# Moving the first norm's scale ahead of the last row blocks of the queries' projection, and ScalarE's first table load ahead of the first tile

## The chip, the core and the metric

The kernel runs on one core of a Trainium2 chip. The metric is the device time of one execution in microseconds (us). The engines are TensorE (PE, matrix multiply; PEld is its weight load), VectorE (DVE), ScalarE (ACT), GpSimd (POOL) and SyncE (SP, which here only issues DMAs). Each engine works through its own instructions in order and waits on semaphores for the others.

## The reference

Two layers of a decoder trunk on a 512 x 2048 input. Only the opening of the first layer matters here: a root-mean-square norm, one wide projection whose columns are split into parts, and a rotary embedding of the queries `b_q` and the keys `b_k`.

```python
def rms_norm(x, w, eps=NORM_EPS):
    xf = x.astype(jnp.float32)
    xf = xf * lax.rsqrt(jnp.mean(xf * xf, axis=-1, keepdims=True) + eps)
    return xf.astype(x.dtype) * w

h = rms_norm(x, pre_w)
proj = h @ w_in
...
qb = apply_rope(b_q.reshape(B, S, SW_HEADS, SW_HEAD_DIM), cos4, sin4)
kb = apply_rope(b_k.reshape(B, S, SW_KV_HEADS, SW_HEAD_DIM), cos4, sin4)
lam = (jnp.exp(jnp.sum(lq1 * lk1)) - jnp.exp(jnp.sum(lq2 * lk2)) + lam_init)
```

## The kernel before

Every product is made of three matmuls, since both factors are held as a high and a low part (`three`, L309): high x high, high x low, low x high. The high part of a weight tile, `whi`, is a cast on ScalarE (L151); the low part, `wlo`, is a subtraction (L152), on VectorE for even row blocks and on POOL for odd ones. The input is treated alike: `act_hi` on ScalarE (L154), `act_lo` on VectorE (L155). Rings limit how far this runs ahead: three raw weight tiles of two row blocks each, and four `whi` and `wlo`, so the cast of a row block needs the matmuls of the fourth block before it to be done.

The first layer opens with the queries' projection (L617). `gemm_tok` runs over 16 row blocks k of 128 rows of `w_in`; for each it adds to four PSUM banks `g` of 128 tokens x 512 columns, 12 matmuls to a block, so 192 in all. `sweep` (L316) orders them: `tail=2` holds the last two blocks back and runs them as one group, bank by bank, so that bank 0 is complete before the others. `before=start` calls `start(k)` (L1062) ahead of each block. It loads the input tiles `xt` by DMA on SP's queue (limited by N_LOAD), splits them (`take`, limited by N_TAKE), squares them on ScalarE and adds the squares up in `ssum` on VectorE (`square`, L1044), and moves the rotary tables forward by a step of VectorE work (`angles`, L206 to L238).

The norm's scale is not applied to the input but to what comes out. When the 16th square is added, `first_scale` (L1055) is queued on the lanes, a small planner that `sweep` calls after each group; it yields L_FIRST first, which puts it behind the last group. It sums `ssum` over partitions by four small products on TensorE (`css`, `col_sums` L454), and VectorE makes `r_in` by a Newton iteration (`rsqrt`, L157). Then VectorE scales the rotary tables (L281) and rotates the queries bank by bank (`rotate_q`, L249 to L259); L253 is the last reader of a bank. The next product (L624: the rotary key, keys and values, 16 blocks of 320 columns, here called kv0 to kv15) needs the same four banks: its first group takes kv0 and kv1 bank by bank, six matmuls to a bank, and so follows the rotations. Between the rotations and the rest of that product stands `layer_constants` (L484): four small DMAs of `lam_in` on SP's queue, products and sums on VectorE (L498, L499) and an exponential on ScalarE (L500), behind which later casts of `kv` tiles are queued.

ScalarE's first instruction that needs a function table is the split of the first input tile (L154).

Of the kernel before, what the change touches and what calls it, by code (L numbers as in the profile page):

```python
# [12 lines left out]
F32 = mybir.dt.float32  # L13
F32R = mybir.dt.float32r
I32 = mybir.dt.int32
AF = mybir.ActivationFunctionType
# [3 lines left out]
P = 128  # L20
# [12 lines left out]
B_Q, B_K, B_G = 2048, 3072, 3328  # L33
# [75 lines left out]
def trunk(ctx: ExitStack, tc: tile.TileContext, ins, inv_freq, out):  # L109
    nc = tc.nc  # L110
    PS = bass.MemoryType.PSUM
    const = ctx.enter_context(tc.tile_pool(name="const", bufs=1))
# [20 lines left out]
    A = nc.scalar  # L133
# [32 lines left out]
        return y  # L166


    ident = const.tile([P, P], F32, name="ident")
    make_identity(nc, ident)  # L170
    act_hi = const.tile([P, 2, KT, 256], F32R, name="act_hi")
    act_lo = const.tile([P, 2, KT, 256], F32R, name="act_lo")
    ones_r = const.tile([P, P], F32R, name="ones_r")
    ones_f = const.tile([P, 2], F32, name="ones_f")
    nc.gpsimd.memset(ones_f, 1.0)
    A.activation(ones_r, ident, AF.Copy, scale=0.0, bias=1.0)
    causal = const.tile([P, S], F32, name="causal")
    nc.gpsimd.memset(causal, 0.0)
    nc.gpsimd.affine_select(out=causal[:, 384:512], in_=causal[:, 384:512], pattern=[[-1, P]],
# [96 lines left out]
    def scaled_tables(r, half, to):  # L276

        mm_ = slice(2 * half, 2 * half + 2)
        rb = r[:, mm_].rearrange("p (m o) -> p m o", o=1).broadcast_to([P, 2, 64])
        for src, dst in zip(tabs, to):  # L280
            V.tensor_tensor(dst[:, mm_, :], src[:, mm_, :], rb, op=ALU.mult)  # L281
# [4 lines left out]
    def stream(w, segs, nk, C, rows=0, before=None):  # L286

        for k0 in range(0, nk, 2):
            raw = wraw.tile([P, 2, S], F32, name="raw", tag="raw")
            c = 0  # L290
            for off, width in segs:
                for j, n in ((0, 1), (1, 1)) if opening[0] else ((0, 2),):
                    nc.sync.dma_start(
                        out=raw[:, j:j + n, c:c + width],
                        in_=w[rows + (k0 + j) * P:rows + (k0 + j + n) * P, off:off + width].rearrange(
                            "(k p) c -> p k c", p=P))
                opening[0] = False
                c += width
            for i in range(2):
                if before:  # L300
                    before(rows // P + k0 + i)
                hi = wsp.tile([P, S], F32R, name="whi", tag="whi")[:, 0:C]
                lo = wsp.tile([P, S], F32R, name="wlo", tag="wlo")[:, 0:C]
                with (tc.high_priority() if ahead[0] or last_rows[0] else nullcontext()):
                    split(hi, lo, raw[:, i, 0:C], behind=behind[0], E=nc.gpsimd if ahead[0] or (i and not last_rows[0]) else V)
                behind[0] = False
                yield k0 + i, hi, lo

    def three(out_ap, a, b, first, last):  # L309

        (ah, al), (bh, bl) = a, b
        mm(out_ap, ah, bh, start=first, stop=False)
        mm(out_ap, ah, bl, start=False, stop=False)
        mm(out_ap, al, bh, start=False, stop=last)

    def sweep(tiles, nk, jobs, after=None, tail=2, head=True):  # L316

        def run(group):  # L320
            for job in jobs:
                for n, t in group:
                    job(t, n == 0, n == nk - 1)
                if fine[0] and job is not jobs[-1]:
                    lanes.tick()
            for n, t in group:
                if after:
                    after(n)
            lanes.tick()

        held = []
        for n, t in enumerate(tiles):
            held.append((n, t))
            if (n == 0 and head) or nk - tail <= n < nk - 1:
                continue
            run(held)
            held = []
# [12 lines left out]
    def gbanks(n):  # L350
        return [psg.tile([P, S], F32, name="g", tag="g") for _ in range(n)]

    def gemm_tok(block, w, segs, C, nk=KT, ms=range(NB), kruns=None, before=None, tail=2, head=True):

        ps = gbanks(len(ms))

        def tiles():
            for k0, cnt in kruns or ((0, nk),):
                for k, hi, lo in stream(w, segs, cnt, C, k0 * P, before):
                    yield k0 + k, hi, lo  # L360

        sweep(tiles(), nk, [lambda t, a, z, p=p, m=m: three(p[:, 0:C], block(t[0], m), t[1:], a, z)
                            for p, m in zip(ps, ms)], tail=tail, head=head)
        return ps
# [119 lines left out]
    def layer_constants(l, cols):  # L484
        c = dict(qnw=cols[:, KT:KT + 4], kvnw=cols[:, KT + 4:KT + 8])
        lam_init = 0.8 - 0.6 * math.exp(-0.3 * l)
        sub = layer_c.tile([P, 1], F32, name=f"sub{l}")
        V.tensor_scalar(sub, cols[:, KT + 8:KT + 9], 0.5 * (1.0 - lam_init), None, op0=ALU.mult)
        sink = layer_c.tile([P, 16], F32, name=f"sink{l}")
        nsink = layer_c.tile([P, 16], F32, name=f"nsink{l}")  # L490
        late(nc.sync.dma_start(out=sink, in_=ins["sink_logits"][l].partition_broadcast(P)))
        V.tensor_scalar(nsink, sink, -1.0, None, op0=ALU.mult)
        lt = slot("lam_in", "et", shape=(P, 4, 64))
        for i, n in enumerate(("q1", "k1", "q2", "k2")):
            late(nc.sync.dma_start(out=lt[:, i, :], in_=ins["diff_lambda_" + n][l].partition_broadcast(P)))
        d, junk = sm("lam_d", 2), slot("lam_j", "et", shape=(P, 64))
        for i in range(2):
            V.tensor_tensor(junk, lt[:, 2 * i, :], lt[:, 2 * i + 1, :], op=ALU.mult)  # L498
            V.tensor_reduce(d[:, i:i + 1], junk, axis=AX.X, op=ALU.add)  # L499
        A.activation(d, d, AF.Exp)  # L500
        nlam = layer_c.tile([P, 1], F32, name=f"nlam{l}")
        V.tensor_tensor(nlam, d[:, 1:2], d[:, 0:1], op=ALU.subtract)
        V.tensor_scalar(nlam, nlam, -lam_init, None, op0=ALU.add)
        c.update(sub=sub, sink=sink, nsink=nsink, nlam=nlam)
        return c
# [54 lines left out]
    def layer(l, pre, norms, r_in, start=None):  # L560
# [3 lines left out]
        w_in, w_out, w_uq, w_ukv = (ins[n][l] for n in ("w_in", "w_out", "w_uq", "w_ukv"))  # L564
# [12 lines left out]
        def fed(half, k):  # L577
            tasks, done, _ = norms[half]
            lanes.finish_until(lambda: min(done) > k // 4,
                               lambda: any(t is q for t in tasks for q in lanes.queue))  # L580
# [14 lines left out]
        def rotate_q(ps, m):  # L595
            d = slot("q_rot", "rot")
            rope(d, ps, m, 8, rtabs)
            return d
# [15 lines left out]

        kv_segs = [(C_KR, 64), (B_K, 256)]
        if start:
            ps = gemm_tok(act_block, w_in, [(B_Q, 512)], 512, before=start, head=False)  # L617
            lanes.finish(*norms)
            for half in range(2):
                scaled_tables(r_in, half, rtabs)  # L620
            for m in range(NB):
                qt[0][m] = rotate_q(ps[m], m)
            c = layer_constants(l, pre)
            kd = key_tiles(gemm_tok(act_block, w_in, kv_segs, 320, tail=3), range(NB), None)  # L624
            keys += [lanes.add(key_half, half, kd[2 * half:2 * half + 2]) for half in range(2)]
        for half in range(0 if start else 2):
            ms = (2 * half, 2 * half + 1)
            ps = gemm_tok(act_block, w_in, kv_segs, 320, ms=ms, before=lambda k: fed(half, k))
# [6 lines left out]
            ps = gemm_tok(act_block, w_in, [(B_Q, 512)], 512, ms=ms)  # L635
# [100 lines left out]
        ps = gemm_tok(act_block, w_in, [(B_Q + 512, 512)], 512)  # L736
# [43 lines left out]
        ps = gemm_T(act, w_in, [(C_Q, S)])  # L780
        qh, ql, ssum = latent(ps, c["qnw"])
        scales = [lanes.add(q_scale, ssum)]
        ps = gemm_T(act, w_in, [(C_KV, S)])
# [4 lines left out]
        ps = gemm_tok(lambda k, m: cut((qh[k], ql[k]), m), w_uq, [(192 * h + 128, 64) for h in range(4)], 256, nk=4)  # L788
# [154 lines left out]
        for h in range(4):  # L943
            ps = gemm_tok(
                act_block, w_in, [(A_K + 128 * h, 128), (A_Q + 128 * h, 128), (A_V + 128 * h, 128)], 384)
# [8 lines left out]
            for m in range(NB):  # L954
                A.activation(raw[:, :, m, :], ps[m][:, 0:384].rearrange("p (k c) -> p k c", k=3), AF.Copy,
                             scale=r_in[:, m:m + 1])
# [96 lines left out]
            norms.append(lanes.add(first_scale))  # L1053

    def first_scale(lane):  # L1055
        yield L_FIRST
        ms = sm("ms")
        V.tensor_scalar(ms, col_sums(bank("css", lane), ssum), 1.0 / DM, EPS, op0=ALU.mult, op1=ALU.add)
        V.tensor_copy(r_in, rsqrt(ms, "rin"))
        yield 0.0  # L1060

    def start(k):  # L1062
        while loaded[0] < min(2 * k + 3, k + N_LOAD, KT):
            load(loaded[0])
            loaded[0] += 1
        while taken[0] < min(k + 1 if k < 2 else 2 * k, k + N_TAKE, KT):
            take(taken[0])
# [22 lines left out]
L_SW = 5.0  # L1090
L_MLA = 7.0
L_DA = 4.5
N_LOAD = 6
N_TAKE = 3
L_FIRST = 2.0
L_KEYS = 5.0
L_SCALE = 1.0
L_FEED = 4.0
# [32 lines left out]
```

## Time and profile before

| | |
|---|---|
| median of 3 runs | 1769.45 us (1768.54 to 1769.94) |
| profiled execution, time | 1767.51 us |
| its span, first to last instruction | 1765.7 us |
| mean granted TensorE clock | 0.993 |
| TensorE busy with matmuls | 1719.0 us, 97% |
| VectorE, ScalarE, POOL busy | 51%, 46%, 42% |

The engine with the most work is TensorE; what is left to gain is in the stretches where it stands still or runs at a lower clock. A timeline row gives start and duration in us, engine, line, operation, result and operands; a bracket at its end tells how long the engine had been idle and what ended the wait. Durations of neighbouring instructions overlap a little, so the distance between two starts is what an instruction costs its engine.

### The profile page before, as it was taken

How to read it: one execution, taken by the hardware profiler on the slowest of the kernel's cores; microseconds unless marked ns; L12 is line 12 of the kernel's file. 1: busy time of each engine (PE TensorE's matmuls, PEld its weight loads, DVE VectorE, ACT ScalarE, POOL GpSimd, SP SyncE). 2: the span in 40 equal slices, each digit the busy share in tenths (PEclk: the TensorE clock that was granted, in tenths of full speed). 3: DMA queues.
4: the chain of work that ended last, by engine and by line, in shares of the span. 5: the costliest groups of instructions: out<-in, count | busy, mean ns of one | idle time of the engine just before them, and what ended most of it. 6: DMA issues, size and time to landing. Idle time of an engine off the chain costs nothing. (4 is left out here: it accounts for less than half of the span.)

```text
span 1765.7 us, 24988 instructions
## 1 busy us (share of the span) xinstructions
PE 1719.0 (97%) x8776; PEld 1478.0 (84%) x8776; DVE 899.5 (51%) x2216; ACT 803.5 (46%) x1744; POOL 746.6 (42%) x630
## 2 busy tenths in 40 slices
PE   8899999999999999999989999999999999999997
PEld 6888888888999988887777888888889999888885
DVE  8445625653435767202785563365625367671035
ACT  6244525544334445235554453355434344552353
POOL 3243443443444444457434434433434434444550
PEclk9999999999999999999999999999999999999998
DMA  6332232232323233336765323222323322332366
GB/s 199 81 95 78 84 101 84 64 104 72 107 78 80 72 111 115 110 107 193 230 188 168 96 84 96 84 84 75 98 68 111 83 71 74 118 131 87 117 207 222
DMA packets 155918, 195.42 MB, mean 111 GB/s; under 512 B 22144, under 2 KB 81552, under 8 KB 155792
## 3 DMA queue, kind: packets, MB, share of 16 engines
q1 hardware_dynamic: 152384, 183.31, 34.8%
q0 software_dynamic: 3264, 10.51, 1.7%
q8 instruction: 69, 1.13, 0.3%
q14 instruction: 57, 0.47, 0.1%
q10 hardware_dynamic: 144, 0.01, 0.0%
HBM read 181.20 MB, written 12.58 MB: 110 GB/s over the span
## 5 line engine op out<-in xcount | busy, mean ns | idle before, releaser
L152 POOL TENSOR_TENSOR wlo<-raw,whi 128x512 fp32r<-128x512 f32 (+3 forms) x576 | 721.9, 1261 | 932.3 <-ACT whi L151 905.0
L151 ACT CAST whi<-raw 128x512 fp32r<-128x512 f32 (+2 forms) x672 | 388.9, 583 | 626.5 <-PE g L142 481.4
L142 PE MATMUL g<-whi,act_hi 128*128 128x512 f32 (+2 forms) x1408 | 525.1, 373 | 12.5 <-ACT whi L151 6.9
L142 PE MATMUL g<-wlo,act_hi 128*128 128x512 f32 (+2 forms) x1408 | 520.2, 369 | 13.3 <-DVE wlo L152 11.8
L142 PE MATMUL g<-whi,act_lo 128*128 128x512 f32 (+2 forms) x1408 | 517.7, 368 | 0.0
L142 PE MATMUL g<-act_hi,whi 128*128 128x512 f32 x768 | 310.9, 405 | 1.7 <-DVE vl L155 0.6
L142 PEld LDWEIGHTS g<-wlo,act_hi 128*128 128x128 f32 x1408 | 266.4, 189 | 54.2 <-DVE wlo L152 16.9
L142 PEld LDWEIGHTS g<-whi,act_hi 128*128 128x128 f32 x1408 | 266.4, 189 | 48.8 <-ACT whi L151 7.4
L142 PE MATMUL g<-act_hi,wlo 128*128 128x512 f32 x768 | 303.7, 395 | 0.1
L142 PE MATMUL g<-act_lo,whi 128*128 128x512 f32 x768 | 303.4, 395 | 0.0
L142 PEld LDWEIGHTS g<-whi,act_lo 128*128 128x128 f32 x1408 | 266.1, 189 | 34.6
L142 PEld LDWEIGHTS g<-act_hi,wlo 128*128 128x128 f32 x768 | 144.3, 188 | 35.1 <-POOL wlo L152 0.5
L142 PEld LDWEIGHTS g<-act_hi,whi 128*128 128x128 f32 x768 | 144.6, 188 | 32.5 <-DVE vl L155 1.5
L142 PEld LDWEIGHTS g<-act_lo,whi 128*128 128x128 f32 x768 | 144.7, 188 | 29.1
L152 DVE TENSOR_TENSOR pTl<-pT,pTh 128x512 fp32r<-128x512 f32 (+2 forms) x112 | 68.2, 611 | 96.4 <-ACT pTh L151 96.2
L987 DVE TENSOR_TENSOR ob<-g,post_norm_w 128x512 f32<-128x512 f32 x32 | 22.1, 690 | 177.4 <-ACT sq L985 177.4
L152 DVE TENSOR_TENSOR wlo<-raw,whi 128x512 fp32r<-128x512 f32 (+1 forms) x96 | 66.2, 695 | 90.1 <-ACT whi L151 90.0
L151 ACT CAST pTh<-pT 128x512 fp32r<-128x512 f32 (+2 forms) x112 | 58.6, 525 | 46.0 <-PE pT L146 45.1
L446 DVE CUSTOM_DVE_ANT_0 p<-sc,causal 128x128 f32<-128x128 f32 (+3 forms) x96 | 46.0, 479 | 33.9 <-PE sc L142 33.9
L146 PE MATMUL pT<-ident,p 128*128 128x128 f32 x384 | 61.0, 274 | 1.4 <-DVE p L852 1.4
L661 ACT ACTIVATE p<-p,nm 128x256 f32<-128x256 f32 (+1 forms) x128 | 59.9, 469 | 0.0
L448 ACT ACTIVATE p<-p,nm 128x128 f32<-128x128 f32 (+3 forms) x64 | 36.0, 562 | 49.7 <-DVE nm L447 49.7
(236 smaller groups left out, 2009.7 us busy)
## 6 DMA issues: line engine op xcount, KB each, us to landing
raw<-w_in SPq DMA_DIRECT2D x135, 512.0 KB, 3.7
raw<-w_out SPq DMA_DIRECT2D x96, 512.0 KB, 3.8
raw<-w_in SPq DMA_DIRECT2D x192, 128.0 KB, 2.4
raw<-w_in SPq DMA_DIRECT2D x26, 256.0 KB, 3.0
xt<-x_t SPq DMA_DIRECT2D x16, 256.0 KB, 6.8
y_spill<-gate POOLq DMA_DIRECT2D x16, 256.0 KB, 2.9
raw<-w_ukv SPq DMA_DIRECT2D x8, 512.0 KB, 3.8
yb<-y_spill POOLq DMA_DIRECT2D x16, 256.0 KB, 3.9
```

The lines of the kernel that those rows point to most:

```text
L142: nc.tensor.matmul(out_, a, b, start=start, stop=stop, skip_group_check=True)
L146: nc.tensor.transpose(out_, in_, ident)
L151: late(A.copy(hi, src), behind)
L152: E.tensor_tensor(lo, src, hi.bitcast(F32), op=ALU.subtract)
L446: V.tensor_tensor_reduce(p, scores, mask, 1.0, -3e38, op0=ALU.add, op1=ALU.max, accum_out=mx)
L448: A.activation(p, p, AF.Exp, bias=nm, scale=scale, accum_out=den)
L661: A.activation(blocks[i], blocks[i], AF.Exp, bias=nm[:, i:i + 1], scale=64.0 ** -0.5, accum_out=den[:, i:i + 1])
L987: V.tensor_tensor(ob[n][m], t, post[n], op=ALU.mult)
```

## The change

`tail=3` holds the last three row blocks of the queries' projection together, blocks 13 to 15. N_TAKE goes from 3 to 4 and N_LOAD from 6 to 7, so that each input tile is loaded, split and squared up to a block sooner and the 16th square is added before block 12's matmuls. `first_scale` loses its L_FIRST yield. Together these put the `css` products behind block 12 (the thirteenth) and ahead of the group of 13, 14 and 15. Separately, `ones_r` is now made at the very start by a copy from `ones_f`, so ScalarE's first table load stands ahead of that copy and no longer ahead of the first tile's split.

```diff
--- before.py
+++ after.py
@@ -166,14 +166,14 @@
         return y
 
 
+    ones_r = const.tile([P, P], F32R, name="ones_r")
+    ones_f = const.tile([P, 2], F32, name="ones_f")
+    nc.gpsimd.memset(ones_f, 1.0)
+    A.copy(ones_r, ones_f[:, 0:1].broadcast_to([P, P]))
     ident = const.tile([P, P], F32, name="ident")
     make_identity(nc, ident)
     act_hi = const.tile([P, 2, KT, 256], F32R, name="act_hi")
     act_lo = const.tile([P, 2, KT, 256], F32R, name="act_lo")
-    ones_r = const.tile([P, P], F32R, name="ones_r")
-    ones_f = const.tile([P, 2], F32, name="ones_f")
-    nc.gpsimd.memset(ones_f, 1.0)
-    A.activation(ones_r, ident, AF.Copy, scale=0.0, bias=1.0)
     causal = const.tile([P, S], F32, name="causal")
     nc.gpsimd.memset(causal, 0.0)
     nc.gpsimd.affine_select(out=causal[:, 384:512], in_=causal[:, 384:512], pattern=[[-1, P]],
@@ -614,7 +614,7 @@
 
         kv_segs = [(C_KR, 64), (B_K, 256)]
         if start:
-            ps = gemm_tok(act_block, w_in, [(B_Q, 512)], 512, before=start, head=False)
+            ps = gemm_tok(act_block, w_in, [(B_Q, 512)], 512, before=start, tail=3, head=False)
             lanes.finish(*norms)
             for half in range(2):
                 scaled_tables(r_in, half, rtabs)
@@ -1053,7 +1053,6 @@
             norms.append(lanes.add(first_scale))
 
     def first_scale(lane):
-        yield L_FIRST
         ms = sm("ms")
         V.tensor_scalar(ms, col_sums(bank("css", lane), ssum), 1.0 / DM, EPS, op0=ALU.mult, op1=ALU.add)
         V.tensor_copy(r_in, rsqrt(ms, "rin"))
@@ -1090,9 +1089,8 @@
 L_SW = 5.0
 L_MLA = 7.0
 L_DA = 4.5
-N_LOAD = 6
-N_TAKE = 3
-L_FIRST = 2.0
+N_LOAD = 7
+N_TAKE = 4
 L_KEYS = 5.0
 L_SCALE = 1.0
 L_FEED = 4.0
```

On TensorE, at the end of the queries' projection, before (`g_132` to `g_135` are the queries' banks, `g_632` the next product's first):

```order
L142 MATMUL g_135<-whi_534,act_hi_88 128x512
L142 MATMUL g_135<-wlo_535,act_hi_88 128x512
L142 MATMUL g_135<-whi_534,act_lo_89 128x512
L142 MATMUL css_563<-ones_f_91,ssum_115 128x2 x4
L142 MATMUL g_632<-whi_639,act_hi_88 128x320
```

and now:

```order
L142 MATMUL g_135<-wlo_497,act_hi_92 128x512
L142 MATMUL g_135<-whi_496,act_lo_93 128x512
L142 MATMUL css_513<-ones_f_84,ssum_115 128x2 x4
L142 MATMUL g_132<-whi_533,act_hi_92 128x512
L142 MATMUL g_132<-wlo_534,act_hi_92 128x512
```

The column sums, once behind all 192 matmuls, have 36 of them behind them.

On VectorE, around the low half of block 12, before (`wlo_492` is block 12's):

```order
L227 SCALAR_TENSOR_TENSOR angles_169<-angles_169 128x128
L1051 TENSOR_TENSOR ssum_115<-ssum_115,sq_488 128x512
L227 SCALAR_TENSOR_TENSOR angles_169<-angles_169 128x128
L152 TENSOR_TENSOR wlo_492<-raw_484,whi_491 128x512
L227 SCALAR_TENSOR_TENSOR angles_169<-angles_169 128x128
L155 SCALAR_TENSOR_TENSOR act_lo_89<-xt_440,cols0_113,act_hi_88 128x2x256
L229 TENSOR_SCALAR angles_169<-angles_169 128x128
L1051 TENSOR_TENSOR ssum_115<-ssum_115,sq_509 128x512
L230 TENSOR_SCALAR angles_169<-angles_169 128x128
```

and now (`wlo_497` is block 12's):

```order
L227 SCALAR_TENSOR_TENSOR angles_169<-angles_169 128x128
L1051 TENSOR_TENSOR ssum_115<-ssum_115,sq_470 128x512
L227 SCALAR_TENSOR_TENSOR angles_169<-angles_169 128x128
L155 SCALAR_TENSOR_TENSOR act_lo_93<-xt_416,cols0_113,act_hi_92 128x2x256
L227 SCALAR_TENSOR_TENSOR angles_169<-angles_169 128x128
L1051 TENSOR_TENSOR ssum_115<-ssum_115,sq_493 128x512
L229 TENSOR_SCALAR angles_169<-angles_169 128x128
L152 TENSOR_TENSOR wlo_497<-raw_489,whi_496 128x512
L230 TENSOR_SCALAR angles_169<-angles_169 128x128
```

One split of an input tile, one addition to `ssum` and two steps of the angles that stood behind block 12's `wlo` now stand ahead of it. Blocks 6, 8 and 10 have likewise some such steps more ahead of their `wlo`.

On ScalarE, in the next product, a piece of the difference (`whi` of 128x320 are kv0, kv1, ...):

```order
 L235 ACTIVATE cos<-angles 128x4x32
 L151 CAST whi<-raw 128x512 x2
-L151 CAST whi<-raw 128x320 x7
+L151 CAST whi<-raw 128x320 x6
 L500 ACT_TABLE_LOAD
 L500 ACTIVATE lam_d<-lam_d 128x2
-L151 CAST whi<-raw 128x320 x9
+L151 CAST whi<-raw 128x320 x10
```

The exponential for lambda now stands ahead of the cast of kv6, not of kv7. On SP's queue the `lam_in` loads likewise move ahead of one more weight tile (kv8 and kv9), and stay behind that of kv6 and kv7.

## Rows read from the trace of the kernel before

**Rows 1.** Waits of TensorE, 0 to 120 us: us in total, times, longest us.

```profile
PE g L142 <- DVE q_rot L253: 5.2, 1, 5.2
PE g L142 <- DVE wlo L152: 1.0, 1, 1.0
```

**Rows 2.** Stretch, length; busy PE, PEld, DVE, ACT, POOL; granted clock, DMA share, GB/s.

```profile
24.00:28.00 4.00, 4.00 (x19) 3.22 (x18) 4.00 (x11) 2.40 (x4) 0.02 (x1) 1.00 0.66 202
...
61.00:65.30 4.30, 4.30 (x14) 3.71 (x15) 4.30 (x10) 0.00 (x0) 0.00 (x0) 0.50 0.02 5
...
70.00:80.00 10.00, 10.00 (x70) 10.00 (x69) 2.38 (x7) 3.60 (x8) 2.63 (x3) 1.00 0.37 98
```

**Rows 3.** Timeline, TensorE, end of the queries' projection: start, duration, [idle before].

```profile
54.73 0.95 PE L142 MATMUL css<-ones_f,ssum 128*128 128x2 f32 x8
60.91 0.60 PE L142 MATMUL g<-whi,act_hi 128*128 128x320 f32 x1 [5.23 <-DVE q_rot L253]
...
66.50 0.39 PE L142 MATMUL g<-whi,act_hi 128*128 128x320 f32 x1 [0.44 <-DVE rh L463]
```

**Rows 4.** Timeline, TensorE, row blocks 8 and 12 of the queries.

```profile
32.47 0.50 PE L142 MATMUL g<-wlo,act_hi 128*128 128x512 f32 x1 [0.96 <-DVE wlo L152]
...
43.77 0.40 PE L142 MATMUL g<-wlo,act_hi 128*128 128x512 f32 x1
```

**Rows 5.** Timeline, VectorE, the queries' row blocks 2 and 12.

```profile
12.54 0.69 DVE L152 TENSOR_TENSOR wlo<-raw,whi 128x512 fp32r<-128x512 f32 x1 [0.81 <-ACT whi L151]
...
42.84 0.68 DVE L152 TENSOR_TENSOR wlo<-raw,whi 128x512 fp32r<-128x512 f32 x1
43.44 0.28 DVE L227 SCALAR_TENSOR_TENSOR angles<-angles 128x128 f32<-128x128 f32 x1
...
45.04 0.21 DVE L230 TENSOR_SCALAR angles<-angles 128x128 f32<-128x128 f32 x1
```

**Rows 6.** Timeline, VectorE, the first norm's scale and the first rotations.

```profile
54.73 0.49 DVE L152 TENSOR_TENSOR wlo<-raw,whi 128x320 fp32r<-128x320 f32 x1 [5.79 <-ACT whi L151]
55.72 0.16 DVE L1058 TENSOR_SCALAR ms<-css 128x4 f32<-128x4 f32 x1 [0.50 <-PE css L142]
...
56.64 0.16 DVE L163 TENSOR_TENSOR rsq_u<-rin 128x4 f32<-128x4 f32 x1
...
59.43 0.42 DVE L249 TENSOR_TENSOR rope<-g,rsin 128x256 f32<-128x256 f32 x1
...
65.68 0.68 DVE L253 TENSOR_TENSOR q_rot<-g,rcos 128x512 f32<-128x512 f32 x1
```

**Rows 7.** Timelines, POOL, VectorE and ScalarE: splitting weight tiles.

```profile
18.08 3.50 POOL L152 TENSOR_TENSOR wlo<-raw,whi 128x512 fp32r<-128x512 f32 x1 [3.67 <-ACT whi L151]
...
55.52 0.86 POOL L152 TENSOR_TENSOR wlo<-raw,whi 128x320 fp32r<-128x320 f32 x1 [4.72 <-ACT whi L151]
...
47.62 1.32 DVE L152 TENSOR_TENSOR wlo<-raw,whi 128x320 fp32r<-128x320 f32 x1 [0.19 <-ACT whi L151]
...
54.23 0.46 ACT L151 CAST whi<-raw 128x320 fp32r<-128x320 f32 x1 [4.38 <-PE g L142]
```

**Rows 8.** Timeline, TensorE, another column sum (css) in a running stream.

```profile
359.79 0.95 PE L142 MATMUL css<-ones_f,ssum 128*128 128x2 f32 x8
...
360.91 0.39 PE L142 MATMUL g<-act_lo,whi 128*128 128x512 f32 x1
```

**Rows 9.** Timeline, TensorE, its longest wait for a wlo.

```profile
905.03 0.80 PE L142 MATMUL g<-wlo,act_hi 128*128 128x512 f32 x1 [2.70 <-DVE wlo L152]
```

**Rows 10.** Timeline, ScalarE, the program's start.

```profile
3.86 1.28 ACT L154 ACT_TABLE_LOAD   x1 [3.86 <-DMA xt<-x_t]
5.16 0.72 ACT L154 ACTIVATE act_hi<-xt,cols 128x512 fp32r<-128x512 f32 x1
```

**Rows 11.** Timelines, SP's queue and ScalarE, the lambda inputs.

```profile
63.59 0.34 SPq L495 DMA_DIRECT2D lam_in<-diff_lambda_q  x1
...
71.19 0.20 ACT L500 ACTIVATE lam_d<-lam_d 128x2 f32<-128x2 f32 x1
```

## The prediction

> **What bounds the kernel now.** I read the waits of TensorE first, over the opening 120 us, since the change touches nothing behind that and TensorE is 97% busy over the whole span. There the reader is to see one wait of 5.2 us on `q_rot` (L253) and one of 1.0 us on a `wlo` [rows 1]. The timeline then shows what the 5.2 us are [rows 3]: the last matmul of the queries' projection is issued just before 54.73, the column sums follow, and the first matmul of the next product comes at 60.91, when bank 0 has been rotated. From there TensorE goes at the pace of the rotations, bank by bank, and reaches bank 3 at 66.50, again behind a wait of 0.44. It runs at the lower clock in between (granted 0.50, the level of 1.2 GHz) after the idle time, and at full clock later [rows 2]; that loss lies under the rotations, so it is not to be counted again. Behind 66.50 TensorE is full, 10.00 of 10.00 us from 70 to 80 [rows 2]. So **the time at which bank 3 of the next product starts, 66.50 now, is the quantity to predict**: what it gains, the whole program gains.
>
> VectorE sets it: the sums arrive at 55.72, the iteration and the tables take until 59.43, and four rotations until the last L253, which starts at 65.68 [rows 6].
>
> The third view is the stretch from 12.54 to 45.6. VectorE stands at 4.00 of 4.00 us there, and TensorE does as well [rows 2], and the timeline of VectorE has no idle time from 12.54 on [rows 5]. At 12.54 it had waited for a cast, and that cast for a weight tile's DMA. Two engines are full at once, then, and work moved forward on VectorE can hold TensorE up.
>
> **The change part by part.**
>
> *The first table load.* It starts at 3.86 when the input tile lands, and the first split follows at 5.16 [rows 10]. Ahead of the copy of `ones_r` it lies under the DMA, so the first split may start up to 1.3 us sooner (5.16 less 3.86), and the first matmul as much, or less if the weight tile, whose landing the trace doesn't tell, comes late. I count nothing for it: the DMAs are as before up to the tile that VectorE waits for at 12.54, from there VectorE is full, and the next step shows that TensorE then runs into VectorE. The removed copy from `ident` costs nothing now, since ScalarE waited for that same DMA behind it.
>
> *The steps moved ahead of block 12's low half.* Before, that `wlo` starts at 42.84 and is ready at 43.52; TensorE takes it at 43.77 [rows 4, 5], so it had 0.25 us to spare. Now four steps that stood between 43.44 and 45.04 stand ahead of it: 1.60 us [rows 5]. With VectorE full, the `wlo` is ready at 45.12 and TensorE takes it at about 45.19, **1.42 us later** than before. This holds whether or not TensorE began earlier. Without waits TensorE would get there at 43.77 less the 0.96 and some 1.2, at 41.6; the difference of 3.6 us becomes waits for `wlo` at blocks 4, 6, 8 and 12, of 0.6, 1.2, 1.2 and 0.6 by the same counting of steps.
>
> *The column sums.* Blocks 8 and 12 are 48 matmuls apart and 11.30 us, 0.235 us each [rows 4]. Eleven more matmuls end block 12 at 47.78. No wait of their own is added: the last addition to `ssum` stands ahead of block 12's `wlo` on VectorE. Before, their issue lay in TensorE's idle time. Now 36 matmuls are queued behind them. In a running stream such sums take 1.12 us up to the second matmul after them [rows 8], less one matmul 0.89. So the group of 13 to 15 starts at 48.67 and ends, 36 x 0.235 = 8.46 later, at 57.13, against 54.73 before.
>
> *The scale and the rotations.* The sums reach VectorE 0.99 us after they start (55.72 less 54.73) [rows 3, 6]: 48.77. To L163 it is 0.92, then kv0's `wlo` now stands in between, 0.49, then 2.79 to the first rotation, which starts at 52.97; bank 0 has been complete since 48.67 + 9 x 0.235 = 50.8, and the others keep ahead likewise. The last L253 starts 6.25 later, ends 0.68 after that at 59.90 [rows 6], and TensorE follows 0.14 behind (66.50 less 66.36): 60.04. For its part TensorE reaches bank 3 at 57.13 and 18 matmuls of 0.143 (10 us by 70) [rows 2], 59.70, with banks 0 to 2 free in time: bank 0 is free after a quarter of the 6.93 at most, 54.7.
>
> *What is held up behind the larger group.* Block 13's `whi` is now used until its last three matmuls in bank 3, at about 55.7, and kv1 takes its place in the ring. Its cast takes 0.46 and its `wlo` on POOL 0.86 [rows 7]: ready at 57.1, needed at 57.13 + 4 x 0.143 = 57.7. Now this falls into the rotations. Under a full VectorE one POOL `wlo` took 3.50 us [rows 7]; 0.86 us scaled to 512 columns would be 1.38, so 2.1 us came on top. Conversely a VectorE `wlo` of 0.49 took 1.32 beside POOL's: 0.83 lost [rows 6, 7]. Between nothing and 0.83 I take 0.35, since POOL's work is only 320 columns wide and there is one such: bank 3 at **60.4**. If POOL is the one held up, kv1 comes at 59.2, 1.5 late, and bank 3 at 61.2.
>
> In this row pair both engines lose while they run together, whatever their operands. The Trainium skill (GPSIMD Engine Reference, Specifications) says that POOL shares its SBUF interfaces with VectorE and contends with instructions in a two-port mode or with two SBUF inputs. Three of the four instructions of a rotation read `g` from PSUM and only one SBUF input, so by that rule little would be lost here; bank 3 would come at 60.0 and the time would be 0.4 us lower.
>
> *The lambda chain.* The `lam_in` loads wait for the second rotation's last addition, before at 63.59 and 4.16 behind the first L249; the exponential ends 7.80 later [rows 6, 11]. Now that is 52.97 + 4.16 + 0.35 = 57.5, or up to 59.2 if the load of kv6 and kv7 ahead of it on SP waits for kv1's `wlo`. It ends at 65.3 to 67.0, and kv6's cast and `wlo` queued behind it 0.95 later, at 66.3 to 68.0. TensorE needs kv6 at 60.4 + (6 + 48 + 1) x 0.143 = 68.3. It is just covered; a later landing would be paid in full. kv4's `wlo`, behind the first lambda product on VectorE, has a similar cover.
>
> *The sum.* 66.50 - 60.4 = **6.1 us** gained: 5.2 + 0.4 of waits and the drain of the banks go, 1.4 and 0.9 come back in the projection. The profiled execution took 1767.51 (span 1765.7 and 1.8 around it), so 1761.4 for one like it; the median of the runs stands 1.94 above it, so the predicted time is 1769.45 - 6.1 = 1763.3.
>
> **The rivals.**
>
> *VectorE is not the pace.* If the moved steps cost TensorE nothing, because VectorE has slack that the trace doesn't show, the group ends 1.4 us sooner and the rest with it: 7.5 us, or 7.9 without the 0.35: 1761.5. Against it: the `wlo` of block 8 already came 0.96 late [rows 4].
>
> *The gain is taken back in the next product.* kv1 to kv3 and the lambda chain all become just-in-time, where they had 5 us before. If kv1 comes 1.5 late (0.8 on bank 3) and kv6 waits as much as the chain can slip behind it (1.7), and one more POOL `wlo` stalls VectorE (0.83), 6.1 shrinks to 2.8: 1766.7, within what the measurement can tell from nothing.
>
> *Slower by the clock.* TensorE's waits grow from one to four. After one of 2.70 us the next matmul took 0.80 us [rows 9], after one of 0.96 us 0.50 [rows 4], and after the 5.2 us the clock stood at its lower level for the 4.3 us to 65.3 [rows 2]. If the wait at block 12, at 45.2, is the one that lets the clock fall and it stays at the lower level through block 12, the group of 36 and the first group of the next product, 47 matmuls take twice their 0.235 and 24 twice their 0.143: 14.5 us more, and the 6.1 turn into a loss of 8.4: 1777.9. It decides from a wait between 0.96 and 2.70; mine are 1.2 at most, and 4.3 us are less than the 14 that this needs, which speaks against it. A drop before block 12 is absorbed, since VectorE sets the pace there.
>
> *The change doesn't do what it says*: the sums would have to come late enough that TensorE waits for `q_rot` all the same, at 1769. The order on VectorE excludes it unless they come 2.4 us later (57.13 against 54.7).
>
> **How the numbers follow.** Forecast, 0.68. VectorE not the pace, 0.10. Gain taken back to under 3.5 us, with the last rival, 0.17. Slower by the clock, 0.05. A measurement of this kernel tells about 0.2%, 3.5 us, from no change. So faster 0.78, same 0.17, slower 0.05. The range reaches from the first rival with half a microsecond of scatter, 1761.0, to the second, 1766.7; the upper end also covers one POOL stall more in the full stretch.
>
> **What would show it.** In the changed kernel's trace: the 5.2 us on `q_rot` gone; in its place three to five waits on `wlo` before 46 us, together 3 to 4 us; the column sums near 47.8; the last matmul of the projection near 57, later than before; bank 3 of the next product at 60 to 61 with a granted clock of 1.00 throughout; the first split near 4.0. It is wrong if TensorE reaches the column sums well before 47, or if new waits of over 1 us stand between 61 and 80.

## The result, and the profile after

The changed kernel takes **1741.98 us** (median of 4 runs, 1740.08 to 1743.55) against 1768.99 for the kernel before beside it (4 runs, 1767.04 to 1769.94). The ratio is 0.985, with a 95% interval of 0.9838 to 0.9862: 27.0 us faster, where 6.1 were forecast. The time lies 19 us below the lower end of the range.

The opening went nearly as forecast. TensorE's waits from 0 to 120 us in the kernel after (us in total, times, longest):

```profile
PE g L142 <- DVE wlo L152: 3.3, 3, 1.2
PE g L142 <- DVE q_rot L253: 0.5, 1, 0.5
```

The 5.2 us on `q_rot` of [rows 1] are gone, and three waits on `wlo` stand in their place. TensorE's timeline in the kernel after:

```profile
26.90 0.50 PE L142 MATMUL g<-wlo,act_hi 128*128 128x512 f32 x1 [1.19 <-DVE wlo L152]
...
33.75 0.50 PE L142 MATMUL g<-wlo,act_hi 128*128 128x512 f32 x1 [1.10 <-DVE wlo L152]
...
40.53 0.50 PE L142 MATMUL g<-wlo,act_hi 128*128 128x512 f32 x1 [1.00 <-DVE wlo L152]
...
48.60 0.95 PE L142 MATMUL css<-ones_f,ssum 128*128 128x2 f32 x8
49.41 0.49 PE L142 MATMUL g<-whi,act_hi 128*128 128x512 f32 x1
49.73 0.40 PE L142 MATMUL g<-wlo,act_hi 128*128 128x512 f32 x1
...
57.71 0.30 PE L142 MATMUL g<-whi,act_hi 128*128 128x320 f32 x1
...
61.01 0.39 PE L142 MATMUL g<-whi,act_hi 128*128 128x320 f32 x1 [0.47 <-DVE q_rot L253]
```

The last row is bank 3 of the next product: 61.01 against 66.50 in [rows 3], 5.5 us sooner. The profiled execution is 1741.76 against 1767.51, so it gained 25.8. **Some 20 us came from somewhere else.** The page's first line of busy times, of the kernel before and then of the kernel after, says from which engine:

```profile
PE 1719.0 (97%) x8776; PEld 1478.0 (84%) x8776; DVE 899.5 (51%) x2216; ACT 803.5 (46%) x1744; POOL 746.6 (42%) x630
```

```profile
PE 1695.7 (97%) x8776; PEld 1478.0 (85%) x8776; DVE 903.7 (52%) x2216; ACT 803.8 (46%) x1744; POOL 742.9 (43%) x630
```

The same 8776 matmuls keep TensorE busy for 23.3 us less; its idle time falls by only 2.4 (the span falls by 25.7, from 1765.7 to 1740.0). The gain lies in the products of 512 columns, in every stage that has them. Here are the same two groups of instructions, of before and then of after (busy time, mean ns of one, idle time ahead):

```profile
L142 PE MATMUL g<-act_hi,wlo 128*128 128x512 f32 x768 | 303.7, 395 | 0.1
L142 PE MATMUL g<-act_lo,whi 128*128 128x512 f32 x768 | 303.4, 395 | 0.0
```

```profile
L142 PE MATMUL g<-act_hi,wlo 128*128 128x512 f32 x768 | 300.2, 391 | 0.1
L142 PE MATMUL g<-act_lo,whi 128*128 128x512 f32 x768 | 299.6, 390 | 0.0
```

A stretch in which TensorE never waits shows it best. In the last product of the program, 1620 to 1720 us (busy TensorE and how many matmuls, granted clock, DMA share, GB/s), before and then after:

```profile
1620.00:1720.00 100.00, 100.00 (x430) 1.00 0.46 149
```

```profile
1620.00:1720.00 100.00, 100.00 (x443) 1.00 0.63 204
```

At the same granted clock of 1.00, 100 us hold 443 matmuls of 512 columns where they held 430, 3% more. The timeline there, eleven rows apart in each kernel, is the same thing in single instructions; before, then after:

```profile
1629.82 0.39 PE L142 MATMUL g<-wlo,act_hi 128*128 128x512 f32 x1
...
1632.38 0.40 PE L142 MATMUL g<-whi,act_hi 128*128 128x512 f32 x1
```

```profile
1629.77 0.39 PE L142 MATMUL g<-whi,act_hi 128*128 128x512 f32 x1
...
1632.27 0.39 PE L142 MATMUL g<-whi,act_lo 128*128 128x512 f32 x1
```

2.56 us over eleven distances is 0.233 each, 2.50 is 0.227. Over the whole trace, the mean distance of the starts of neighbouring 512-column matmuls of one shape (those under 0.3 us apart, some 4,600 pairs) is 233.2 ns before and 228.1 ns after. I call it the matmul distance below. 4,600 times 5.1 ns are 23 us, nearly all of the busy time that went. The products with `act_hi` or `act_lo` of 384 columns, the next in number, go only from 177.6 to 176.8 ns.

What the change did to these matmuls is not in the order of instructions. Tiles get their place in SBUF in the order in which they are declared, each rounded up to 32 bytes, and the diff declares `ones_r` and `ones_f` ahead of `act_hi` and `act_lo`. The places (bytes from the start of a partition) in the built programs:

```
            before    after
ones_r       82560    16512
ones_f       83072    17024
ident        16512    17056
act_hi       17024    17568
act_lo       49792    50336
whi         211104   211104   and every 2048 bytes, four times
wlo         219296   219296   and every 2048 bytes, four times
```

All but a few of the large products take one operand from `act_hi` or `act_lo` and the other from `whi` or `wlo`. All slices of these start whole multiples of 512 bytes apart, so one number tells how the two operands lie to each other. `whi` less `act_hi` is 194080 before, 32 bytes more than a multiple of 256, and 193536 after, a multiple of 1024. The 32 bytes are `ones_f`, which holds 8 and is rounded up.

The few others are a control. They take `ch` or `cl`, tiles declared behind `act_lo`, in place of `act_hi` or `act_lo`, and `ch` and `cl` lie a multiple of 2048 bytes from `whi` and `wlo` in both kernels. They are as fast before as after:

```profile
L142 PE MATMUL g<-ch,wlo 128*128 128x512 f32 x64 | 25.0, 390 | 0.0
```

```profile
L142 PE MATMUL g<-ch,wlo 128*128 128x512 f32 x64 | 25.0, 391 | 0.0
```

### The profile page after: what moved, and what is told of

It is laid out like the page before. It is cut to its first block, busy times and chain, and to the rows that moved or that the text cites. A ratio compares the mean times of both kernels' runs of the same rounds, so it can differ in the third digit from the quotient of the medians.

```text
span 1740.0 us, 24993 instructions
## 1 busy us (share of the span) xinstructions
PE 1695.7 (97%) x8776; PEld 1478.0 (85%) x8776; DVE 903.7 (52%) x2216; ACT 803.8 (46%) x1744; POOL 742.9 (43%) x630
## 5 line engine op out<-in xcount | busy, mean ns | idle before, releaser
L142 PE MATMUL g<-act_hi,wlo 128*128 128x512 f32 x768 | 300.2, 391 | 0.1
L142 PE MATMUL g<-act_lo,whi 128*128 128x512 f32 x768 | 299.6, 390 | 0.0
```

The lines of the kernel that those rows point to most:

```text
L142: nc.tensor.matmul(out_, a, b, start=start, stop=stop, skip_group_check=True)
```

## The experiments

Each time is a median of 4 runs or more, with the kernel before run beside it.

### Placement and order apart

The kernel before, with nothing but the declarations moved:

```diff
+    ones_r = const.tile([P, P], F32R, name="ones_r")
+    ones_f = const.tile([P, 2], F32, name="ones_f")
     ident = const.tile([P, P], F32, name="ident")
-    make_identity(nc, ident)
     act_hi = const.tile([P, 2, KT, 256], F32R, name="act_hi")
     act_lo = const.tile([P, 2, KT, 256], F32R, name="act_lo")
-    ones_r = const.tile([P, P], F32R, name="ones_r")
-    ones_f = const.tile([P, 2], F32, name="ones_f")
+    make_identity(nc, ident)
     nc.gpsimd.memset(ones_f, 1.0)
     A.activation(ones_r, ident, AF.Copy, scale=0.0, bias=1.0)
```

> The kernel before, with every instruction in its old order; only the declarations of ones_r and ones_f stand ahead of ident, act_hi and act_lo, so those three lie 544 bytes higher in SBUF: act_hi starts at byte 17568 of a partition instead of 17024, an odd multiple of 32 as whi (211104) and wlo are. Placement theory: the 128x512 matmuls come 0.227 us apart instead of 0.233, and some 20 us of the 27 are gained: about 1748. Schedule theory (all of the 27 us come from the changed order): 1769, as before.

Measured: 1747.55 us (1745.58 to 1749.6), ratio 0.9876 (0.9858 to 0.9893), 21.8 us faster than before. The matmul distance is 228.1 ns. TensorE's timeline and its stretch at the end:

```profile
54.00 0.95 PE L142 MATMUL css<-ones_f,ssum 128*128 128x2 f32 x8
60.20 0.60 PE L142 MATMUL g<-whi,act_hi 128*128 128x320 f32 x1 [5.25 <-DVE q_rot L253]
```

```profile
1620.00:1720.00 100.00, 100.00 (x443) 1.00 0.61 197
```

The opening is that of the kernel before, with its wait of 5.2 us [rows 3], and the time falls by 21.8 us all the same. TensorE is busy for 1696.4 us, 22.6 less; 1.1 of it comes back as idle time.

The kernel after, with the old places:

```diff
-    ones_r = const.tile([P, P], F32R, name="ones_r")
-    ones_f = const.tile([P, 2], F32, name="ones_f")
-    nc.gpsimd.memset(ones_f, 1.0)
-    A.copy(ones_r, ones_f[:, 0:1].broadcast_to([P, P]))
     ident = const.tile([P, P], F32, name="ident")
-    make_identity(nc, ident)
     act_hi = const.tile([P, 2, KT, 256], F32R, name="act_hi")
     act_lo = const.tile([P, 2, KT, 256], F32R, name="act_lo")
+    ones_r = const.tile([P, P], F32R, name="ones_r")
+    ones_f = const.tile([P, 2], F32, name="ones_f")
+    nc.gpsimd.memset(ones_f, 1.0)
+    A.copy(ones_r, ones_f[:, 0:1].broadcast_to([P, P]))
+    make_identity(nc, ident)
```

> The changed kernel with every instruction in its new order; only the placement of ident, act_hi, act_lo, ones_r and ones_f is that of before (act_hi at byte 17024). Placement theory: the matmuls are 0.233 us apart again, and only the start is better, by the 5.5 us by which bank 3 of the second product starts sooner in the changed kernel's trace (61.01 against 66.50): about 1763.5. Schedule theory: about 1742, as the changed kernel.

Measured: 1762.98 us (1760.58 to 1765.26), ratio 0.9962 (0.9948 to 0.9975), 6.4 us faster than before; the distance is 233.2 ns. TensorE's timeline:

```profile
48.48 0.95 PE L142 MATMUL css<-ones_f,ssum 128*128 128x2 f32 x8
...
57.78 0.31 PE L142 MATMUL g<-whi,act_hi 128*128 128x320 f32 x1
...
60.42 0.31 PE L142 MATMUL g<-whi,act_hi 128*128 128x320 f32 x1
```

**This is the kernel that the prediction describes**: 1763.3 and bank 3 at 60.4 were forecast. The two parts add up, 21.8 and 6.4 to 28.2, against 27.0 measured for the whole.

Other engines' traffic is not what slows the matmuls. From 52 to 56 us ScalarE, POOL and the DMA stand still in the kernel after and in the one with the old places. Here is that stretch, in this order (columns as in [rows 2]):

```profile
52.00:56.00 4.00, 4.00 (x19) 3.30 (x19) 3.90 (x14) 0.00 (x0) 0.00 (x0) 1.00 0.00 0
```

```profile
52.00:56.00 4.00, 4.00 (x19) 3.22 (x18) 3.93 (x13) 0.00 (x0) 0.00 (x0) 1.00 0.00 0
```

The distance there is 226.7 and 233.3 ns. VectorE, which works in both, isn't what does it either: from 52 to 54 us in the kernel before, VectorE, ScalarE and POOL are idle and it is 233.1. All that TensorE reads there are `act_hi` or `act_lo` and `whi` or `wlo`.

### What about the place counts

The four kernels so far could also be told apart by where `act_hi` alone lies: at a multiple of 64 before, 32 past one after. Two more complete the square. The first leaves 32 bytes ahead of `ident`, so that all later tiles move together:

```diff
     ones_f = const.tile([P, 2], F32, name="ones_f")
+    gap = const.tile([P, 2], F32, name="gap")
     nc.gpsimd.memset(ones_f, 1.0)
+    nc.gpsimd.memset(gap, 0.0)
```

> The changed kernel with 32 bytes more ahead of ident, so that act_hi (17600) and all that lies behind it, whi (211136) too, start at multiples of 64. Both operands of the large matmuls then have the same offset within 64 bytes, as in the changed kernel, but it is 0 and not 32. If the equal offset counts: about 1742 and 0.227 us between matmuls. If act_hi at an odd multiple of 32 counts by itself: 0.233 us and about 1763.

The second leaves them behind `act_lo`, so that `act_hi` and `act_lo` stay where the kernel after has them and all else moves on:

```diff
     act_lo = const.tile([P, 2, KT, 256], F32R, name="act_lo")
+    gap = const.tile([P, 2], F32, name="gap")
+    nc.gpsimd.memset(gap, 0.0)
```

> The changed kernel with 32 bytes more behind act_lo, so that act_hi stays at an odd multiple of 32 (17568) and whi and wlo go to multiples of 64 (211136). If the equal offset of both operands within 64 bytes counts: 0.233 us between matmuls and about 1763. If act_hi at an odd multiple of 32 counts by itself: 0.227 us and about 1742.

Measured: 1742.07 us (1740.76 to 1742.41), ratio 0.9843 (0.9828 to 0.9858), and 1763.75 us (1758.07 to 1764.91), ratio 0.9962 (0.9944 to 0.998); distances 228.1 and 233.2 ns. So it is not the place of `act_hi` by itself that counts but how the two operands lie to each other, and 8 unused bytes in the wrong spot cost 22 us.

The same edit with 64, 128 and 96 bytes (`[P, 16]`, `[P, 32]`, `[P, 24]`) asks which distances are good:

> The kernel after, with 64 bytes left free behind act_lo, so that whi and wlo lie 64 bytes further on; in all kernels so far the operands of the large products lay either a multiple of 1024 bytes apart (fast) or that and 32 more or less (slow). Theory: only the offset within 64 bytes has to be equal. Then 512-column matmuls start 0.227 us apart, as in the kernel after, and the time is 1742 us. Rival: a longer period counts (128 bytes up to 1024). Then they start 0.234 apart and the time is 1763; a distance below 0.227 would say that the placement of after is not the best.

> The kernel after, with 128 bytes left free behind act_lo. So far the distance between the operands of the large products, less whole multiples of 512 bytes, was 0 (matmuls 0.228 us apart on average), 32 (0.233) and 64 (0.231). Theory: a difference costs less the larger the power of two that it is, and 128 lies between 64 and 0: 0.229 to 0.230, 1745 to 1750 us. Rival: all distances off the multiple of 512 cost about as much as 64 or more: 0.231 and over, 1753 us and over. Second rival: only distances that are no multiple of 128 cost: 0.228, 1742 us.

> The kernel after, with 96 bytes left free behind act_lo. Distances of 32, 64 and 128 bytes gave matmuls 0.233, 0.231 and 0.2325 us apart. Theory: every distance that is no multiple of a period of 256 or 512 costs 3 to 5 ns: 0.231 to 0.233, 1753 to 1763 us. Rival: only an even number of 32 bytes that is small costs less, and an odd one costs what 32 costs: 0.2332, 1763 us. A distance at 0.228 would overturn both.

And two ways to shift by more without any gap. `ident` declared behind `act_lo` gives 512:

```diff
-    ident = const.tile([P, P], F32, name="ident")
-    make_identity(nc, ident)
     act_hi = const.tile([P, 2, KT, 256], F32R, name="act_hi")
     act_lo = const.tile([P, 2, KT, 256], F32R, name="act_lo")
+    ident = const.tile([P, P], F32, name="ident")
+    make_identity(nc, ident)
```

> The kernel after, with ident's 512 bytes declared behind act_lo instead of ahead of act_hi, so that the operands of the large products lie 512 bytes off a multiple of 1024; the order of all instructions is that of the kernel after. Theory: 512 bytes are a whole period, since the kernel before (544 off) and the run with a 32-byte gap behind act_lo (32 off) had the same 0.233: matmuls 0.228 us apart, 1742 us. Rival: the period is 1024 or more, and 512 costs something: 0.229 and over, 1745 us and over.

The two tables `cols`, 128 bytes each, taken from the pool of `act_lo` instead of one behind the weight tiles, give 256:

```diff
-        t = layer_c.tile([P, KT + 9], F32, name=f"cols{l}")
+        t = const.tile([P, KT + 9], F32, name=f"cols{l}")
```

> The kernel after, with its two small tables of columns (128 bytes each) declared in the pool of act_lo instead of behind the weight tiles, so that the operands of the large products lie 256 bytes off a multiple of 512; the order of all instructions is that of the kernel after. Theory: 512 is the shortest period, and 256 off costs as 32, 64 and 128 do: 0.231 to 0.233 us between matmuls, 1753 to 1763 us. Rival: 256 is a period: 0.228, 1742 us.

Measured, with the distance of the two operands less whole multiples of 1024 bytes (by this count the kernel before is at 544, not at 32 as the expectation for 64 bytes has it; 544 below is the new order with the old places):

```
operands   matmul distance   time, us (range)              ratio to before
0 (after)  228.1 ns          1741.98 (1740.08-1743.55)     0.9838-0.9862
32         233.2 ns          1763.75 (1758.07-1764.91)     0.9944-0.998
64         231.2 ns          1753.06 (1750.74-1754.02)     0.9898-0.9928
96         233.6 ns          1764.93 (1762.72-1768.87)     0.9975-0.9993
128        232.5 ns          1760.41 (1760.01-1763.82)     0.9943-0.9972
256        228.1 ns          1741.01 (1740.79-1742.25)     0.9834-0.9867
512        228.1 ns          1742.44 (1741.34-1742.81)     0.9838-0.9867
544        233.2 ns          1762.98 (1760.58-1765.26)     0.9948-0.9975
```

The stretch from 1620 to 1720 us of the kernels with 64, 128 and 256:

```profile
1620.00:1720.00 100.00, 100.00 (x439) 1.00 0.56 181
```

```profile
1620.00:1720.00 100.00, 100.00 (x432) 1.00 0.52 166
```

```profile
1620.00:1720.00 100.00, 100.00 (x443) 1.00 0.64 208
```

My first theory, that equal places within 64 bytes are enough, fell with 64: 1753 and not 1742. The one after it, that a shift costs less the larger the power of two it is, fell with 128, which is slower than 64; that 512 would be the shortest period fell with 256. 96 costs about what 32 does, as its rival had it. What stands is that 0, 256 and 512 are alike to 0.1 ns, and every distance tried between costs 3 to 5.5 ns a matmul. 32 and 544 are alike too, so 256 bytes as a period fit all that was tried; 160, 192 and 224 were not tried, nor any that is no multiple of 32. Why two operands that lie unequally slow each other down no run shows. None of the places is better than that of the kernel after.

### The terms of the opening

The kernel after with the table loaded late, `ones_r` made from `ident` as before, at the same place:

```diff
-    A.copy(ones_r, ones_f[:, 0:1].broadcast_to([P, P]))
...
+    A.activation(ones_r, ident, AF.Copy, scale=0.0, bias=1.0)
```

> The kernel after, with ones_r made where it was before (from ident, behind the first tiles), so that ScalarE's table is loaded when the first tile has landed; every tile stays where the kernel after has it. Theory: the first matmul comes some 1.2 us later (6.4 for 5.20), the waits for wlo shrink by as much, and the column sums come at 48.6 as in the kernel after: 1742 us. Rival: TensorE is the pace of the opening, and all comes 1.2 us later: sums at 49.8, 1743.2 us.

Measured: 1739.6 us (1737.98 to 1741.23), ratio 0.9842 (0.9825 to 0.9858), which this measurement can't tell from the kernel after. TensorE's timeline:

```profile
6.45 0.80 PE L142 MATMUL g<-whi,act_hi 128*128 128x512 f32 x1 [6.45 <-ACT whi L151]
...
26.44 0.50 PE L142 MATMUL g<-wlo,act_hi 128*128 128x512 f32 x1 [1.21 <-DVE wlo L152]
...
48.14 0.95 PE L142 MATMUL css<-ones_f,ssum 128*128 128x2 f32 x8
```

The first matmul comes 1.25 us later than in the kernel after (5.20), and the sums 0.46 sooner. The lead is gone at the 15th matmul, here in the kernel after and then in this run:

```profile
11.70 0.40 PE L142 MATMUL g<-whi,act_lo 128*128 128x512 f32 x1
```

```profile
11.70 0.39 PE L142 MATMUL g<-whi,act_lo 128*128 128x512 f32 x1
```

In the kernel after the matmuls stand 0.43 us apart up to 11.37, the 14th, and in this run only up to 10.06, the 8th, though the granted clock is 1.00 in both from 4 to 12 us. From there VectorE sets the pace, and it is ahead in this run. Its low half of block 2, in the kernel after and then here:

```profile
12.96 0.69 DVE L152 TENSOR_TENSOR wlo<-raw,whi 128x512 fp32r<-128x512 f32 x1 [0.60 <-ACT whi L151]
```

```profile
12.48 0.69 DVE L152 TENSOR_TENSOR wlo<-raw,whi 128x512 fp32r<-128x512 f32 x1 [0.50 <-ACT whi L151]
```

The sums and bank 3 keep this half microsecond; whether the table or chance gave it, one trace of each doesn't tell. I had looked for smaller waits on `wlo`; they are as large, 3.3 in all.

The kernel after with the delay ahead of the first scale put back (`yield 2.0`), so that the sums fall behind the last group:

> The kernel after with the delay of 2.0 us ahead of the first scale, as before, so that the column sums fall behind the last group again; all else, the placement too, as in the kernel after. Theory: the sums start at 48.60 + 36 x 0.228 = 56.8, bank 3 of the next product comes 11.8 us behind them as in the kernel before, at 68.6, 7.6 us later than in the kernel after, with a wait of about 5.2 us on q_rot: 1749.6 us. Rival: what the early sums gain is taken back behind the opening: 1742 to 1744.

Measured: 1748.01 us (1746.48 to 1748.57), ratio 0.9885 (0.987 to 0.9899). TensorE's timeline:

```profile
56.77 0.95 PE L142 MATMUL css<-ones_f,ssum 128*128 128x2 f32 x8
62.96 0.60 PE L142 MATMUL g<-whi,act_hi 128*128 128x320 f32 x1 [5.25 <-DVE q_rot L253]
...
68.55 0.38 PE L142 MATMUL g<-whi,act_hi 128*128 128x320 f32 x1 [0.20 <-DVE rh L463]
```

The wait is back and bank 3 is at 68.55 as expected, 7.5 us behind the kernel after; the span is 6.4 longer. In these two executions about a microsecond is made up behind the opening.

The kernel after with `tail=2`:

> The kernel after with the queries' last group of two row blocks, as before, in place of three; the column sums stay behind row block 12. Block 13 then stands alone ahead of the last group and bank 0 is complete some 2.7 us later than in the kernel after's 50.4 to 51.5, at about 53, and on VectorE four steps that make the diagonals (some 1.1 us) come ahead of the rotations. Theory: VectorE's rotations set bank 3, which comes 1.1 us later than 61.01, at 62.1: 1743 us. Rival: bank 0 is the limit and each rotation waits for its bank: bank 3 at 63 or later, 1744 or more.

Measured: 1743.6 us (1740.61 to 1744.18), ratio 0.9858 (0.9843 to 0.9872). TensorE's timeline:

```profile
49.24 0.95 PE L142 MATMUL css<-ones_f,ssum 128*128 128x2 f32 x8
...
62.65 0.38 PE L142 MATMUL g<-whi,act_hi 128*128 128x320 f32 x1 [0.75 <-DVE q_rot L253]
```

Bank 3 comes 13.4 us behind the sums, against 12.4 in the kernel after. On VectorE, the first of the four steps for the diagonals and the first rotation behind them:

```profile
53.93 0.84 DVE L725 TENSOR_TENSOR r_sq<-r_in 128x4 f32<-128x4 f32 x1
...
55.56 0.42 DVE L249 TENSOR_TENSOR rope<-g,rsin 128x256 f32<-128x256 f32 x1
```

The rotations follow without a wait for a bank, as the first theory has it and its rival not. Its size came out by luck: the four steps took 1.63 us, not 1.1, and 0.65 that the kernel after loses beside POOL (below) is not lost here. The time can't be told from no change.

## Why the prediction was wrong

**The step that failed** stands in its first paragraph: that the change touches nothing behind the opening, and that what the opening gains is what the whole program gains. The matmul distance was taken from [rows 4] and [rows 2] as a constant of the program. The moved declarations were read for the instructions in them, and the place that a declaration gives to every tile behind it was costed at nothing, without a word. That missing term is -21.8 us, measured alone. Nothing in the trace of before could give its sign or size, but the prediction should have said that the tiles move against each other and put a bound on it. None of the four rivals had it.

**The order of work: right, by 6.4 us against 6.1.** That bank 3 came at 60.42 with the old places, against 60.4, is partly luck. The sums were 0.70 late there, the scale took 0.50 less, nothing of the 0.35 was lost beside POOL, and TensorE, which has no wait there, got to bank 3 at its own pace, behind the rotations. The terms in the kernel after, against the forecast for bank 3 of 60.4:

- *The table load* was counted at nothing, and the run with the late table bears it out.
- *The waits on `wlo`*: 3.3 us against 3.6. They fall on blocks 6, 8 and 10, not 4, 6, 8 and 12. The sums come at 48.60, not 47.78: 0.82 late, because of the wait at block 10 that I had not seen.
- *The column sums* cost TensorE 49.73 less 48.60 less one matmul of 0.23, 0.90 against 0.89, and the group of 36 behind them takes 8.21 (to 57.71) against 8.46, the shorter matmul distance. No wait was added.
- *The scale*: 3.70 from `ms` to the first rotation, against 4.20. In the kernel before one of the small steps (L160) took 0.49 where it now takes 0.17; I had carried those 0.32 over and then added the `wlo`.
- *The rotations* lose 0.65 beside POOL, where I took 0.35 between 0 and 0.83. Summed: 60.4 + 0.82 - 0.50 + 0.30 is 61.0, and 61.01 was measured.

This loss has a clear picture. VectorE, and then POOL, in the kernel after:

```profile
57.34 0.42 DVE L251 TENSOR_TENSOR rope<-g,rsin 128x256 f32<-128x256 f32 x1
57.67 0.69 DVE L253 TENSOR_TENSOR q_rot<-g,rcos 128x512 f32<-128x512 f32 x1
...
58.60 1.33 DVE L259 TENSOR_TENSOR q_rot<-q_rot,rope 128x512 f32<-128x512 f32 x1
```

```profile
57.15 1.02 POOL L152 TENSOR_TENSOR wlo<-raw,whi 128x320 fp32r<-128x320 f32 x1 [8.09 <-ACT whi L151]
58.51 0.88 POOL L152 TENSOR_TENSOR wlo<-raw,whi 128x320 fp32r<-128x320 f32 x1 [0.34 <-ACT whi L151]
```

And in the kernel with the new order and the old places, VectorE and then POOL:

```profile
58.49 0.69 DVE L259 TENSOR_TENSOR q_rot<-q_rot,rope 128x512 f32<-128x512 f32 x1
```

```profile
58.57 1.35 POOL L152 TENSOR_TENSOR wlo<-raw,whi 128x320 fp32r<-128x320 f32 x1 [0.51 <-ACT whi L151]
```

L251 and L253, with one operand in PSUM, keep their 0.42 and 0.69 beside POOL. L259, with both in SBUF, takes 1.33 when POOL has started 0.09 ahead, and 0.69 when it starts 0.08 ahead itself; then POOL takes 1.35 in place of 0.88. The Trainium skill (SBUF — State Buffer, Who interferes with whom) says that a VectorE instruction with two SBUF inputs and a POOL instruction that reads SBUF shut each other out, and that whichever starts first decides who waits; these rows agree. So both cases of my range occur, one for each order of start: nothing lost on VectorE, and 0.65, near the upper 0.83. The section of the Trainium skill that the prediction weighed (GPSIMD Engine Reference, Specifications) names the two SBUF inputs too; that little would be lost by it was my reading, and the one instruction in four that has them lost 0.65.

- *The lambda chain and kv1* were just covered, as forecast: `lam_in` is issued at 59.12 (57.5 to 59.2 forecast), the exponential ends at 67.15 (65.3 to 67.0, so 0.15 beyond), and TensorE has no wait over 0.5 us between 61.01 and 80. ScalarE in the kernel after:

```profile
66.95 0.20 ACT L500 ACTIVATE lam_d<-lam_d 128x2 f32<-128x2 f32 x1 [2.97 <-DVE lam_d L499]
67.09 0.82 ACT L151 CAST whi<-raw 128x320 fp32r<-128x320 f32 x2
```

**The rivals.** The gain was not taken back behind the opening: with the late sums the span is 6.4 us longer. VectorE does set the pace in the opening: TensorE waits for three of its `wlo`, and with the late table, where VectorE is 0.48 sooner and TensorE level at 11.70, the sums are 0.46 sooner. The lower clock did not come: behind waits of up to 1.19 us the granted clock is 1.00 from 4 to 130 us.

## What to carry to other kernels

Moving a declaration moves every tile behind it, and an odd 32 bytes between the two operands of the main matmuls cost this kernel 1.2% over its whole length, over three times what the reordering gained. When a change touches declarations, compare where the operands lie before costing the instructions, and afterwards compare the distance of matmul starts in a stretch without waits: one row of 100 us tells it. When a measured gain lies far above the part that was changed, look first at whether the same instructions became faster everywhere.

## What the runs showed of the hardware

- Two matmul operands of 512 columns and 128 x 128 that lie 0, 256 or 512 bytes off a multiple of 1024 from each other in SBUF let matmuls start every 228.1 ns on average; 32, 64, 96 and 128 bytes off it is 233.2, 231.2, 233.6 and 232.5. The granted clock is 1.00 in all these kernels from 1620 to 1720 us, where they hold 442 or 443 matmuls, and 430, 439, 430 and 432. Moving both operands by 32 bytes changed nothing (228.1). The loss is there with no other engine at work (233.1 ns from 52 to 54 us in the kernel before, against 226.7 from 50.6 to 54.6 with the late sums), with DMAs under way in both.
- When a subtraction on POOL and an addition on VectorE, each with both operands in SBUF, start 0.08 to 0.09 us apart, the second takes 0.47 to 0.65 us longer.
